# A two-layer transformer kernel: the experts' up weights loaded as one run of eight rows a partition

## The chip, the cores and the metric

The kernel runs on one NeuronCore of a Trainium2 chip. The metric is the device time of one execution in microseconds. Three runs of the kernel before gave 1952.04, 1953.3 and 1950.11 us, a median of 1952.04 us.

The core has five engines with a queue of instructions each: TensorE (PE; its weight loads are listed as PEld), VectorE (DVE), ScalarE (ACT), GpSimd (POOL) and SyncE (SP), which here only issues DMAs. Sixteen DMA engines move data between HBM and the on-chip memory SBUF, which has 128 partitions. Matrix products land in PSUM.

## The reference, cut to what matters

The program is two blocks of two layers each on a sequence of 256 tokens of 1024 float32 features. The first block has a mixer (convolutions in layer 0, attention in layer 1), a layer norm, and then a mixture of 32 experts of which every token uses two:

```python
h = x.reshape(-1, d)                                   # 256 tokens x 1024 features
# a group (1 of 4) and two of its 8 experts are chosen for each token
gate, up = jnp.split(jnp.matmul(xc, w_up[e]), 2, axis=-1)      # w_up[e]: 1024 x 1024
y = jnp.matmul(jax.nn.silu(gate) * up, w_down[e])              # w_down[e]: 512 x 1024
out = jnp.zeros((t, d), h.dtype).at[tok].add(y * weight)
```

All of the weights are float32 and are used once, so that both layers' expert weights come to 64 x (4 MB + 2 MB). The second block (two attention kinds, a gated feed-forward and a gate per layer) is not touched by the change.

A product over the 1024 features is a sum, and it may be taken in any order, as long as the token's features and the rows of `w_up[e]` are cut in the same way.

## The kernel before, in words

**Stages.** The program runs ten stages one after another: 0 convolutions, 1 experts of layer 0, 2 attention, 3 experts of layer 1, and 4 to 9 the second block.

**Weights.** All large weights are cut into items of 1 MB that go to tiles `w` of 128 partitions x 2048 floats. The list `items` has them in the order of use. `pump` (lines 195 to 208) issues the DMA of the next item on SP's queue (line 205) as soon as some tile of the pools is free, and `done` frees a tile when its last reader has been placed. During the expert stages up to 20 tiles circulate (pools of 7, 6, 4 and 3), so that SP can have many loads under way, over a stage's end too: the first experts' weights are asked for while the stage before still runs, and the next stage's weights while the last experts compute.

**An expert's items.** For each expert there are four items of the up weights and two of the down weights (lines 139 to 143). The function `rows` (line 69) maps row `k*128 + p` of the matrix to partition `p`, chunk `k`. An up item holds two chunks, so that each partition gets two pieces of 4096 bytes that lie 512 KB apart in HBM; the 128 pieces of a chunk lie one after another.

**The tokens' features.** The router (stages 1 and 3) scores the tokens, and `gather_mm` (line 822) picks the up to 32 tokens of each of four experts with matrix products: the stationary operand is a chunk of 128 features of the token matrix `x` (256 tokens as 2 x 128 partitions), the moving one is a 0/1 matrix. The result, features on partitions, tokens along the row, is copied out of PSUM by `put` (line 846) with the layer norm's gain and bias for each feature, which `fv` takes from `fvec`: a table that stage 0 makes by turning the loaded vectors (lines 333 to 335). `up` (line 882) then multiplies chunk after chunk with the weights (line 892); `turn` and `down` follow (lines 901 and 914).

**Order around a stage's start.** The router's last step on PE is the gather for the first four experts: eight products for the first 128 tokens, then, after a short step on DVE, eight for the others. Then comes `up(0)`, whose readings free the first tiles. Products of float32 stand as two records each in the trace, so that eight are 16 records.

Of the kernel before, what the change touches and what calls it, by code (L numbers as in the profile page):

```python
# [10 lines left out]
F32 = mybir.dt.float32  # L11
# [23 lines left out]
LN_MIX_G, LN_MIX_B, LN_FFN_G, LN_FFN_B, NORM = 0, 2, 4, 6, 8  # L35
# [33 lines left out]
def rows(ap):  # L69
    return ap.rearrange("(k p) n -> p k n", p=128)  # L70


@with_exitstack
def tile_kernel(ctx: ExitStack, tc: tile.TileContext, A, out, first=0, last=9):
    nc = tc.nc
    V, S, G, T, Q = nc.vector, nc.scalar, nc.gpsimd, nc.tensor, nc.sync
    NA, NB, NC, ND = 7, 6, 4, 3

    const = ctx.enter_context(tc.tile_pool(name="const", bufs=1))
# [7 lines left out]
    def bank():  # L87
        return psum.tile([128, 512], F32, name="ps", tag="ps")
# [4 lines left out]
    items, halves = [], []  # L93

    def dense(view, kind):
        items.append(view)
        i = len(items) - 1
        if kind in ("cols4", "cols2"):
            k = int(kind[4])
            n = 1024 // k  # L100
            for j in range(2):
                halves.append((i, (k, n), lambda t, j=j, k=k, n=n: t.rearrange("p (k n) -> p k n", k=k)
                               [:, :, j * n:(j + 1) * n]))
        elif kind == "feat":
            for m in range(2):
                halves.append((i, (8, 128), lambda t, m=m: t.rearrange("p (k n) -> p k n", k=8)
                               [:, :, m * 128:(m + 1) * 128]))
        elif kind == "gate":
            halves.append((i, (8, 112), lambda t: t[:, 0:896].rearrange("p (k n) -> p k n", k=8)))
        else:  # L110
            k, n = {"tok": (4, 256), "row": (1, 1024)}[kind]
            for j in range(2):
                halves.append((i, (k, n), lambda t, j=j, k=k: t[:, j * 1024:(j + 1) * 1024]
                               .rearrange("p (k n) -> p k n", k=k)))

    def cols(w, c0, n=256):
        return rows(w)[:, :, c0:c0 + n]

    def out_items(w, pairs=False):
        for j in range(0 if pairs else 2):  # L120
            dense(rows(w)[:, 0:4, j * 512:(j + 1) * 512], "cols4")
        for k in range(0 if pairs else 4, 8, 2):
            dense(rows(w)[:, k:k + 2, :], "cols2")
# [3 lines left out]
    for s in range(first, last + 1):  # L127
        stage_half[s] = len(halves)
        if s == 0:
            for i in range(2):  # L130
                dense(cols(A["even_w_in"][0], 2048 + 256 * i), "feat")
                dense(cols(A["even_w_in"][0], 1536 + 256 * i), "feat")
            for i in range(2):
                for c in (512, 1024, 0):
                    dense(cols(A["even_w_in"][0], c + 256 * i), "feat")
            out_items(A["even_w_out"][0])
        elif s in (1, 3):
            moe_items[s] = len(items)
            for e in range(NE):
                for k in range(4):  # L140
                    items.append(rows(A["expert_w_up"][s // 2, e])[:, 2 * k:2 * k + 2, :])
                for k in range(2):
                    items.append(rows(A["expert_w_down"][s // 2, e])[:, 2 * k:2 * k + 2, :])
        elif s == 2:
            for hg in range(4):
                dense(cols(A["odd_w_qkv"][0], 256 * hg), "feat")
                dense(cols(A["odd_w_qkv"][0], 1024 + 256 * hg), "feat")
                dense(cols(A["odd_w_qkv"][0], 2048 + 256 * hg), "tok")
            out_items(A["odd_w_o"][0])
        elif s == 4:  # L150
            for hg in range(4):
                for j in range(3):
                    dense(cols(A["w_in_ab_2"][0], (hg // 2) * 1536 + (hg % 2) * 256 + 512 * j), "tok")
            out_items(A["w_out_ab_2"][0], True)
        elif s in (5, 8):
            for f in range(NF + 1):
                if f < NF:
                    dense(cols(A["w_ffn_gate_2"][s // 7], 256 * f), "feat")
                    dense(cols(A["w_ffn_up_2"][s // 7], 256 * f), "feat")
                if f:  # L160
                    dense(rows(A["w_ffn_down_2"][s // 7])[:, 2 * f - 2:2 * f, :], "row")
        elif s in (6, 9):
            dense(rows(A["w_ple_proj_2"][s // 9]), "row")
            for u in range(4):
                dense(cols(A["w_ple_gate_2"][s // 9], 256 * u), "feat")
        else:
            w = A["w_in_nsa_2"][0]
            for j, n in enumerate(("k", "v")):
                dense(cols(w, 1024 + 256 * j), "tok")
            for n in ("k", "v"):  # L170
                items.append(A[f"cmp_{n}_w1_2"][0].rearrange("(l p) n -> p l n", p=128))
            for c in (1536, 2048):
                dense(cols(w, c), "tok")
            dense(cols(w, 2496, 112), "gate")
            for c in (0, 256, 1792, 2304, 512, 768):
                dense(cols(w, c), "tok")
            out_items(A["w_out_nsa_2"][0], True)
# [118 lines left out]
    x = const.tile([128, 2, D], F32, name="x")  # L296
# [17 lines left out]
    ident = const.tile([128, 128], F32, name="ident")  # L314
# [4 lines left out]

    fvec = const.tile([128, 8, 14], F32, name="fvec")  # L320

    def vector_loads(vr):
        lo, hi = (0 if first < 4 else 8), (14 if last > 3 else 8)
        for j, n in enumerate(("ln_mix_g", "ln_mix_b", "ln_ffn_g", "ln_ffn_b", "norm_mix_2", "norm_ffn_2",
                               "norm_ple_2")):
            if lo <= 2 * j < hi:
                Q.dma_start(vr[2 * j:2 * j + 2, :], A[n])
        if lo:
            V.memset(vr[0:8, :], 0.0)

        def go():
            ps = bank()
            for k in range(8):
                T.transpose(ps[:, k * 14:k * 14 + hi], vr[0:hi, k * 128:(k + 1) * 128], ident[:hi, :hi])
            V.tensor_copy(fvec[:, :, 0:hi], ps[:, 0:112].rearrange("p (k n) -> p k n", k=8)[:, :, 0:hi])
        return go

    def fv(j):
        return lambda k: fvec[:, k, j:j + 1]
# [201 lines left out]
    def conv_mix():  # L541
        mp = rt["pool"]
        with tc.tile_pool(name="cm", bufs=1, reuse_waits="tile") as cp:
# [9 lines left out]
            Q.dma_start(fvr[36:37, :], A["even_norm_b_b"])  # L553
            pump(1)
            vectors = vector_loads(vr)
            prep = router_loads(0)
            pump()
# [165 lines left out]
    def router(mp):  # L723
# [59 lines left out]
        def first():  # L783
            place(0)
            warm(8)
            gather_mm(pg, 0, dsp[:, 0, 0:4])
# [7 lines left out]
        place(1)  # L794
        warm(2)
        gather_mm(pg, 1, dsp[:, 1, 0:4])
        rt.update(pos=pos, first=pg, dt=dt)

# [23 lines left out]
    def gather_mm(ps, c, dsp):  # L822

        for k in range(8):
            T.matmul(ps[k // 4][:, k % 4 * 128:k % 4 * 128 + 128], x[:, c, k * 128:(k + 1) * 128],
                     dsp.rearrange("p e s -> p (e s)"), start=k % 4 == 0 and c == 0, stop=c == 1,
                     skip_group_check=True)

    def moe(layer):
        stage = 2 * layer + 1  # L830
        with tc.tile_pool(name="wd", bufs=ND, reuse_waits="tile") as wd, \
# [5 lines left out]
            router(mg)  # L837
            base = moe_items[stage]
            acc = [bank() for _ in range(4)]
            gain, bias = fv(LN_MIX_G + layer), fv(LN_MIX_B + layer)  # L840
            xgs, y4s, hts = {}, {}, {}
            dsp = rt["dt"][:, 0:512].rearrange("p (c e s) -> p c e s", c=2, e=8)
            dwt = rt["dt"][:, 512:].rearrange("p (q t) -> p q t", q=2)
# [22 lines left out]
            def gather(g, hb):  # L866
                ps = [bank(), bank()]
                for c in range(2):
                    gather_mm(ps, c, dsp[:, c, 4 * hb:4 * hb + 4])
                gathered(g, hb, ps)  # L870
# [1032 lines left out]
    def second_block():  # L1903
        nonlocal jdent, sm
        with tc.tile_pool(name="b2", bufs=1, reuse_waits="tile") as bp, tc.tile_pool(name="sm2", bufs=2) as sm:
# [20 lines left out]
            if first > 3:  # L1926
                with tc.tile_pool(name="b2c", bufs=1) as cp:
                    vector_loads(cp.tile([14, D], F32, name="vr"))()
                    block2_consts(*[cp.tile([128, D], F32, name=f"consts{j}") for j in range(2)])()
# [31 lines left out]
    if 7 in stage_half:  # L1961
        j = halves[stage_half[7]][0]
        nsa_w1 = {"k": j + 2, "v": j + 3}
    with ExitStack() as es:
        if first < 4:
            rt["pool"] = es.enter_context(tc.tile_pool(name="mp", bufs=1, reuse_waits="tile"))
            for p, n in (("b", NB), ("c", NC)):
                pools[p] = es.enter_context(tc.tile_pool(name="w" + p, bufs=n, reuse_waits="tile"))
                free.extend(p * n)
        for s in range(first, min(last, 3) + 1):  # L1970
            if s == 0:
                conv_mix()
            elif s == 2:
                stick_mix()
            else:
                moe(s // 2)
# [37 lines left out]
```

## Time and profile before

| What | Value |
|---|---|
| time, median of 3 runs | 1952.04 us (1950.11 to 1953.3) |
| the profiled execution | 1952.0 us, of which the span 1950.3 us |
| PE busy | 1638.0 us (84%) |
| DVE, ACT, POOL busy | 781.6, 681.3, 196.3 us |
| moved by DMA | 559.04 MB, mean 287 GB/s |
| issues of expert weights | 256 of up weights, 128 of down weights, 1024 KB each |

The page cuts the span into 40 slices of 48.8 us. The row DMA gives the share in tenths that the 16 DMA engines were busy, and the row GB/s what they moved. The expert stages are the two stretches of slices in which DMA shows 9 throughout: about 160 to 590 us, and 749 to 1180 us. Packets of one DMA engine overlap slightly in the records, so that a share can come out a little above 1.

### The profile page before, as it was taken

How to read it: one execution, taken by the hardware profiler on the slowest of the kernel's cores; microseconds unless marked ns; L12 is line 12 of the kernel's file. 1: busy time of each engine (PE TensorE's matmuls, PEld its weight loads, DVE VectorE, ACT ScalarE, POOL GpSimd, SP SyncE). 2: the span in 40 equal slices, each digit the busy share in tenths (PEclk: the TensorE clock that was granted, in tenths of full speed). 3: DMA queues.
4: the chain of work that ended last, by engine and by line, in shares of the span. 5: the costliest groups of instructions: out<-in, count | busy, mean ns of one | idle time of the engine just before them, and what ended most of it. 6: DMA issues, size and time to landing. Idle time of an engine off the chain costs nothing. (4 is left out here: it accounts for less than half of the span.)

```text
span 1950.3 us, 34572 instructions
## 1 busy us (share of the span) xinstructions
PE 1638.0 (84%) x14717; PEld 1241.2 (64%) x14717; DVE 781.6 (40%) x1569; ACT 681.3 (35%) x1299; POOL 196.3 (10%) x152
## 2 busy tenths in 40 slices
PE   7769767667668999767657778999999998999998
PEld 7756423224226986323324225999999997799998
DVE  5873100001104663100001004666655857666557
ACT  3423111111114663211111114655444646654445
POOL 4721000000001000000000002111000412110001
PEclk9889878778878999977778788999999999999999
DMA  9549999999999659999999999545555463145550
GB/s 299 213 143 394 418 419 418 418 420 418 418 419 349 241 182 362 418 420 419 418 418 419 419 419 310 161 154 179 180 186 178 140 207 112 55 136 195 192 176 23
DMA packets 236570, 559.04 MB, mean 287 GB/s; under 512 B 15563, under 2 KB 124938, under 8 KB 236408
## 3 DMA queue, kind: packets, MB, share of 16 engines
q1 hardware_dynamic: 226520, 551.59, 74.3%
q10 hardware_dynamic: 9264, 4.97, 0.9%
q8 instruction: 119, 1.95, 0.4%
q14 instruction: 43, 0.35, 0.1%
q0 software_dynamic: 624, 0.18, 0.0%
HBM read 555.55 MB, written 1.15 MB: 285 GB/s over the span
## 5 line engine op out<-in xcount | busy, mean ns | idle before, releaser
L892 PE MATMUL ps<-w,xg 128*32 128x256 f32 x4096 | 362.3, 493 | 235.8 <-DMA w<-in_expert_w_up_dram 231.5
L892 PEld LDWEIGHTS ps<-w,xg 128*32 128x32 f32 x4096 | 134.7, 132 | 445.5 <-DMA w<-in_expert_w_up_dram 266.2
L251 DVE TENSOR_TENSOR wl<-w,wh 128x1024 fp32r<-128x1024 f32 x231 | 281.2, 1226 | 157.2 <-ACT wh L240 153.9
L240 ACT ACTIVATE wh<-w 128x1024 fp32r<-128x1024 f32 x273 | 283.5, 1051 | 90.5 <-PE ps L401 60.1
L896 DVE TENSOR_TENSOR hs<-hs,ps 128x128 f32<-128x128 f32 x64 | 18.4, 288 | 631.6 <-ACT hs L895 631.6
L400 PE MATMUL ps<-xh,wh 128*128 128x256 f32 (+1 forms) x840 | 237.1, 282 | 0.0
L402 PE MATMUL ps<-xh,wl 128*128 128x256 f32 (+1 forms) x840 | 236.3, 281 | 0.8 <-DVE wl L251 0.8
L401 PE MATMUL ps<-xl,wh 128*128 128x256 f32 (+1 forms) x840 | 236.6, 282 | 0.4 <-DVE xl L1218 0.3
L895 ACT ACTIVATE hs<-ps 128x128 f32<-128x128 f32 x64 | 17.8, 278 | 591.9 <-PE ps L892 587.2
L251 POOL TENSOR_TENSOR wl<-w,wh 128x1024 fp32r<-128x1024 f32 x42 | 115.5, 2764 | 996.2 <-ACT wh L240 996.2
L402 PEld LDWEIGHTS ps<-xh,wl 128*128 128x128 f32 (+1 forms) x840 | 159.2, 189 | 1.2 <-DVE wl L251 1.2
L401 PEld LDWEIGHTS ps<-xl,wh 128*128 128x128 f32 (+1 forms) x840 | 159.2, 189 | 1.2 <-DVE xl L1218 1.2
L400 PEld LDWEIGHTS ps<-xh,wh 128*128 128x128 f32 (+1 forms) x840 | 159.2, 190 | 0.0
L914 PE MATMUL ps<-w,ht 128*32 128x256 f32 x2048 | 144.9, 432 | 0.0
L921 ACT ACTIVATE y<-ps 32x256 f32<-32x256 f32 x256 | 96.0, 375 | 119.9 <-PE ps L914 113.8
L914 PEld LDWEIGHTS ps<-w,ht 128*32 128x32 f32 x2048 | 74.5, 128 | 67.6 <-issue 35.7
L402 PE MATMUL ps<-wh,xl 128*128 128x256 f32 x352 | 100.4, 285 | 5.0 <-DVE xl L1218 5.0
L400 PE MATMUL ps<-wh,xh 128*128 128x256 f32 x352 | 102.2, 290 | 1.5 <-ACT xh L1215 1.5
L401 PE MATMUL ps<-wl,xh 128*128 128x256 f32 x352 | 99.6, 283 | 0.0
L401 PE MATMUL ps<-al,wh 128*128 128x256 f32 x352 | 99.1, 281 | 0.0
L400 PE MATMUL ps<-ah,wh 128*128 128x256 f32 x352 | 99.0, 281 | 0.0
L402 PE MATMUL ps<-ah,wl 128*128 128x256 f32 x352 | 99.0, 281 | 0.0
(403 smaller groups left out, 2883.5 us busy)
## 6 DMA issues: line engine op xcount, KB each, us to landing
w<-in_expert_w_up_dram SPq DMA_DIRECT2D x256, 1024.0 KB
w<-in_expert_w_down_dram SPq DMA_DIRECT2D x128, 1024.0 KB
w<-in_w_ffn_gate_dram SPq DMA_DIRECT2D x22, 1024.0 KB
w<-in_w_ffn_up_dram SPq DMA_DIRECT2D x22, 1024.0 KB
w<-in_w_ffn_down_dram SPq DMA_DIRECT2D x22, 1024.0 KB
w<-in_odd_w_qkv_dram SPq DMA_DIRECT2D x12, 1024.0 KB
w<-in_w_in_ab_dram SPq DMA_DIRECT2D x12, 1024.0 KB
w<-in_w_in_nsa_dram SPq DMA_DIRECT2D x10, 1024.0 KB
```

Of the source, the lines that this page charges most:

```text
L240: S.activation(hv, src, AF.Copy)
L251: eng.tensor_tensor(out=lv, in0=src, in1=hv.bitcast(F32), op=OP.subtract)
L400: T.matmul(ps, lh, rh, start=start, stop=False, **kw)
L401: T.matmul(ps, lh, rl, start=False, stop=False, **kw)
L402: T.matmul(ps, ll, rh, start=False, stop=stop, **kw)
L892: T.matmul(pu[32 * j:32 * j + 32, 0:256], r, w[:, kk, :, j, :], start=k == 0, stop=k == 7)
L895: S.activation(hs, pu[:, 0:128], AF.Silu)
L896: V.tensor_tensor(out=hs, in0=hs, in1=pu[:, 128:256], op=OP.mult)
L914: T.matmul(pd[32 * c:32 * c + 32, 0:256], hts[e][:, 32 * j:32 * j + 32], w[:, jj, c * 256:(c + 1) * 256], start=j == 0, stop=j == 3)
L921: S.activation(y4s[q][32 * ee:32 * ee + 32, c * 256:(c + 1) * 256], pd[32 * c:32 * c + 32, 0:256], AF.Copy)
```

## The change

The up weights' rows are dealt to the partitions in another way: partition `p` gets the eight neighbouring rows `8p` to `8p+7` (new function `runs`). An item still holds two of the eight, and these are now one piece of 8192 bytes; the next partition's piece lies 32 KB further on. The down weights stay as they are.

Chunk `k` of the features is then `k, k+8, k+16, ...` in place of 128 neighbours. So the gather reads its stationary operand with a step of eight floats (32 bytes), and the gain and bias for the gathered features come from a second small table, `runvec`, which is made by eight further transposes and a copy in stage 0.

```diff
+def runs(ap):
+
+    return ap.rearrange("(p k) n -> p k n", p=128)
...
-                    items.append(rows(A["expert_w_up"][s // 2, e])[:, 2 * k:2 * k + 2, :])
+                    items.append(runs(A["expert_w_up"][s // 2, e])[:, 2 * k:2 * k + 2, :])
...
+    runvec = const.tile([128, 8, 4], F32, name="runvec") if first < 4 else None
...
             V.tensor_copy(fvec[:, :, 0:hi], ps[:, 0:112].rearrange("p (k n) -> p k n", k=8)[:, :, 0:hi])
+            if not lo:
+                ps = bank()
+                for k in range(8):
+                    T.transpose(ps[:, k * 4:k * 4 + 4], vr[0:4, k::8], ident[:4, :4])
+                V.tensor_copy(runvec.rearrange("p k n -> p (k n)"), ps[:, 0:32])
...
     def gather_mm(ps, c, dsp):
...
-            T.matmul(ps[k // 4][:, k % 4 * 128:k % 4 * 128 + 128], x[:, c, k * 128:(k + 1) * 128],
+            T.matmul(ps[k // 4][:, k % 4 * 128:k % 4 * 128 + 128], x[:, c, k::8],
...
-            gain, bias = fv(LN_MIX_G + layer), fv(LN_MIX_B + layer)
+            gain, bias = [lambda k, j=j + layer: runvec[:, k, j:j + 1] for j in (LN_MIX_G, LN_MIX_B)]
```

On SP's queue, where the first experts' weights follow those of stage 0, the kernel before has these rows (the tile `w`, what it is loaded from, and the shape of the access):

```order
L205 DMA w<-in_even_w_in_dram 128x8x256 x6
L205 DMA w<-in_even_w_out_dram 128x4x512 x2
L205 DMA w<-in_even_w_out_dram 128x2x1024 x2
L205 DMA w<-in_expert_w_up_dram 128x2x1024 x4
L205 DMA w<-in_expert_w_down_dram 128x2x1024 x2
```

and the changed one, whose lines of the same functions stand some lines lower, has these:

```order
L210 DMA w<-in_even_w_in_dram 128x8x256 x6
L210 DMA w<-in_even_w_out_dram 128x4x512 x2
L210 DMA w<-in_even_w_out_dram 128x2x1024 x2
L210 DMA w<-in_expert_w_up_dram 128x2048 x4
L210 DMA w<-in_expert_w_down_dram 128x2x1024 x2
```

The number of DMAs and their order are the same; an up item is 128 pieces of 2048 floats in place of 128 x 2 pieces of 1024. On PE in stage 0, between two products of the convolution's input (lines 400 to 402), the table `fvec` is turned out of the loaded vectors `scr`:

```order
L401 MATMUL ps<-w,wh 128x256
L402 MATMUL ps<-w,wl 128x256
L334 MATMUL ps<-ident,scr 128x14 x8
L400 MATMUL ps<-w,wh 128x256
L401 MATMUL ps<-w,wh 128x256
```

and in the changed kernel:

```order
L413 MATMUL ps<-w,wh 128x256
L414 MATMUL ps<-w,wl 128x256
L341 MATMUL ps<-ident,scr 128x14 x8
L346 MATMUL ps<-ident,scr 128x4 x8
L412 MATMUL ps<-w,wh 128x256
L413 MATMUL ps<-w,wh 128x256
```

Eight transposes are added behind the eight that were there, and on DVE one copy behind that of line 335. Elsewhere the instructions and their order are the same; of the gathers and the copies behind them only the addresses change.

## Rows read from the trace of the kernel before

**Rows 1.** The page: the span in 40 slices, and the DMA packets.
```profile
PE   7769767667668999767657778999999998999998
...
DMA  9549999999999659999999999545555463145550
GB/s 299 213 143 394 418 419 418 418 420 418 418 419 349 241 182 362 418 420 419 418 418 419 419 419 310 161 154 179 180 186 178 140 207 112 55 136 195 192 176 23
DMA packets 236570, 559.04 MB, mean 287 GB/s; under 512 B 15563, under 2 KB 124938, under 8 KB 236408
...
q8 instruction: 119, 1.95, 0.4%
q14 instruction: 43, 0.35, 0.1%
```

**Rows 2.** Waits of the whole span: engine, line, releaser, us, times, longest.
```profile
PEld ps L892 <- DMA w<-in_expert_w_up_dram: 266.2, 162, 4.7
PE ps L892 <- DMA w<-in_expert_w_up_dram: 231.5, 186, 6.0
```

**Rows 3.** Busy time by stretch; the last two columns are DMA share and GB/s.
```profile
161.00:575.00 414.00, 297.85 (x3201) 140.81 (x3189) 40.09 (x123) 67.76 (x182) 3.46 (x6) 0.81 1.02 418
300.00:500.00 200.00, 141.39 (x1457) 65.71 (x1457) 19.77 (x53) 29.74 (x82) 0.00 (x0) 0.78 1.03 418
749.00:1170.00 421.00, 300.62 (x3265) 142.67 (x3257) 38.91 (x120) 69.36 (x187) 0.00 (x0) 0.81 1.02 417
622.00:630.00 8.00, 8.00 (x80) 7.79 (x79) 3.42 (x5) 3.24 (x4) 0.00 (x0) 1.00 1.09 386
```

**Rows 4.** DMA issues from 159.3 to 600 us (first two alike in 748 to 1190).
```profile
w<-in_expert_w_up_dram SPq DMA_DIRECT2D x114, 1024.0 KB
w<-in_expert_w_down_dram SPq DMA_DIRECT2D x58, 1024.0 KB
w<-in_odd_w_qkv_dram SPq DMA_DIRECT2D x4, 1024.0 KB
```

**Rows 5.** PE in order of time at stage 1's start: start, us, line, operands, count.
```profile
146.37 1.98 PE L739 MATMUL ps<-rw,xt 128*128 128x36 f32 x16
148.17 1.07 PE L508 MATMUL ps<-ident,x 128*128 128x128 f32 x8
...
153.55 2.05 PE L825 MATMUL ps<-dt,x 128*128 128x128 f32 x16
155.44 0.59 PE L396 MATMUL ps<-onesb 128*128 128x512 bf16 x2
155.87 0.18 PE L777 MATMUL ps<-mb,onesb 128*128 128x32 bf16 x1
...
156.69 2.05 PE L825 MATMUL ps<-dt,x 128*128 128x128 f32 x16 [0.18 <-DVE dt L780]
158.68 3.66 PE L892 MATMUL ps<-w,xg 128*32 128x256 f32 x64
```

**Rows 6.** SP's queue: issues of weights at the two expert stages' starts.
```profile
159.81 1.23 SPq L205 DMA_DIRECT2D w<-in_expert_w_up_dram  x2
161.53 1.26 SPq L205 DMA_DIRECT2D w<-in_expert_w_down_dram  x2
...
748.49 1.23 SPq L205 DMA_DIRECT2D w<-in_expert_w_up_dram  x2
```

**Rows 7.** Busy time by stretch around these issues; last columns DMA share, GB/s.
```profile
155.00:159.00 4.00, 3.82 (x36) 2.88 (x38) 0.91 (x4) 1.11 (x4) 0.88 (x2) 1.00 1.03 416
159.00:160.00 1.00, 1.00 (x25) 0.57 (x21) 1.00 (x4) 0.40 (x2) 0.00 (x0) 1.00 0.22 74
...
748.00:749.00 1.00, 1.00 (x24) 0.62 (x20) 0.84 (x3) 0.98 (x2) 0.00 (x0) 1.00 0.07 29
```

**Rows 8.** PE around 1570 us: products with a moving operand at a step.
```profile
1570.68 4.57 PE L1658 MATMUL ps<-kpk,w 128*128 128x75 f32 x32
1574.98 0.39 PE L400 MATMUL ps<-wh,xh 128*128 128x256 f32 x1
```

**Rows 9.** Weight loads, whole span, shapes apart: busy us, mean ns, idle before.
```profile
L825 PEld LDWEIGHTS ps<-dt,x 128*128 128x128 f32 x512 | 59.4, 193 | 2.1 <-DVE dt L780 2.1
L508 PEld LDWEIGHTS ps<-ident,xn 128*128 128x128 f32 x16 | 1.7, 141 | 0.8 <-DVE xn L496 0.8
L716 PEld LDWEIGHTS ps<-rw,fvec 128*1 128x1 f32 x32 | 1.1, 85 | 0.3
```

**Rows 10.** PE, then DVE, in order of time in stage 0.
```profile
23.84 0.80 PE L334 MATMUL ps<-ident,scr 14*128 14x14 f32 x8
24.57 0.39 PE L400 MATMUL ps<-w,wh 128*128 128x256 f32 x1
...
27.78 0.69 DVE L615 TENSOR_TENSOR gp<-sg,ps 128x512 f32<-128x512 f32 x1 [2.82 <-PE ps L402]
29.20 19.02 DVE L590 SCALAR_TENSOR_TENSOR scr<-gp,vec,scr 128x256 f32<-128x256 f32 x26 [0.73 <-DMA w<-in_even_w_in_dram]
```

**Rows 11.** One stretch late in stage 0.
```profile
100.00:110.00 10.00, 0.00 (x0) 0.00 (x0) 9.42 (x18) 2.80 (x4) 3.39 (x2) 0.64 0.00 0
```

## The prediction

> **What bounds the kernel now.** I read the 40 slices first. In slices 5 to 12 and 17 to 24 the DMA row shows 9 and the GB/s row 418 to 420, while PE shows 6 to 8 [rows 1]: these are the two expert stages, and there the loads are the bound. The waits say the same: PE's products of line 892 waited 231.5 us in all for up weights [rows 2]. By stretch, 161 to 575 and 749 to 1170 us have a DMA share of 1.02 at 417 to 418 GB/s with PE busy for 298 of 414 and 301 of 421 us [rows 3]. So a tile of 1.049 MB takes 1.049/418 = 2.51 us, PE has over a quarter of its time to spare, and what the loads lose or gain in these stretches goes through to the end. Outside them the weights run ahead and PE, or in stage 0 DVE, sets the pace.
>
> **The change, part by part.**
>
> *The loads.* In each stage 114 up tiles are issued after the stretch has begun [rows 4]; the other 14 come earlier, with DMA time to spare. So 228 tiles count. What a longer piece is worth I take from two saturated stretches. Around 626 us only next-stage weights in pieces of 1 KB arrive: 386 GB/s at share 1.09. Between 300 and 500 us everything comes in pieces of 4 KB: 418 GB/s [rows 3]. An engine has a sixteenth of that, so a piece takes 1024 x 16/386 = 42.4 ns and 4096 x 16/418 = 156.8 ns. The line through both has 38.1 ns per KB and 4.3 ns per piece. A piece of 8 KB then takes 309.3 ns against 313.6 for two of 4 KB, 1.4% less: 34 ns a tile, and 228 x 34 ns = 7.8 us gained.
>
> Its ends: the row of before has no load of weights in pieces over 4 KB (only the 162 packets of the two instruction queues are above 8 KB [rows 1]), so nothing shows that SP's queue moves 8 KB as one packet. If not, the gain is 0. If the busy shares are taken for the packets' real time (16 x 1.09/386 gives 46.3 ns per 1 KB, 16 x 1.03/418 gives 161.5 per 4 KB), 8 KB take 315.1 against 323.0 ns, 2.4%: 14 us gained. A loss is possible too, through the new addresses; it is the third rival. I take the middle value, since it goes by bytes that arrived and not by shares over 1.
>
> *The gathers.* 512 records of line 825 [rows 9] now read the stationary operand at a step of 32 bytes. Most of them lie in the stretches where PE waits for weights: a gather of 32 records that grew by 3 us would still be hidden by up to 20 tiles on their way. Only the first gather of each stage counts in full. Its two halves of 16 records stand on PE without a break but for 0.18 us, right before `up(0)` [rows 5], and SP's next loads come only when `up(0)` frees tiles: at 159.8 us, a microsecond after its start at 158.7 [rows 6]; the same holds at 748.5. Just then the DMA has run dry: its share falls from 1.03 to 0.22 at 159 us, and to 0.07 at 748 [rows 7]. So 64 records stand on the path, and each nanosecond more on one is 0.064 us.
>
> What a record costs is set by the weight load: 16 records of line 739 with only 36 moving columns take 148.17 - 146.37 = 1.80 us, 112 ns each, and those of line 825 take 1.89/16 = 118 ns [rows 5]. No weight load at a step is in the trace, so I bound it. Line 1658 reads its moving operand at the same step, eight floats: 32 records in 4.30 us, 134 ns for 75 columns, 1.79 ns a column [rows 8], where line 825 has at most 118/128 = 0.92. A read at this step therefore costs at least 1.94 times as much. If a weight load grows alike, 112 becomes 217 ns and the two first gathers lose 64 x 0.105 = 6.7 us. Against it: a block of the same 128 x 128 floats is loaded for a transpose in 141 ns and for a product in 193, and a single column takes 85 [rows 9]. So reading 128 contiguous columns needs at most 56 ns, and the load for a product takes 108 above the single column; a read 1.94 times as long, 109 ns, would just fit in. I take 0, because these rows are weight loads themselves, and keep 6.7 as the other end. A gain has no ground: the operand has as many columns as before.
>
> [...]
>
> *Stage 0.* The eight transposes of line 334 took 24.57 - 23.84 = 0.73 us on PE. DVE was waiting 2.82 us for PE's next result and then ran unbroken [rows 10]; late in the stage it is DVE that everyone waits for (9.42 of 10 us busy while PE has none) [rows 11]. So eight more delay the chain by about 0.7 us; the bounds are 0, if a later wait takes them up, and 1.5, if the read at a step doubles them. The copy to `runvec` lies in DVE's wait.
>
> *Neither adds nor removes anything:* the copies with gain and bias have the same shapes, and SP issues the same DMAs in the same order.
>
> *Sum:* 1952.0 (the profiled execution: span 1950.3 and 1.7 around it; the median of the runs is 1952.04) - 7.8 + 0 + 0.7 = 1944.9 us, 0.36% less.
>
> **The rivals.**
>
> 1. *The gathers give it back.* The loads gain 7.8 us, but weight loads at a step take 217 ns: -7.8 + 6.7 + 0.7, 1951.6 us. For it speaks line 1658, against it the quick weight loads of the transposes.
>
> 2. *The change doesn't do what it says on the wires.* The queue cuts 8 KB into two packets of 4 KB. The rate stays at 418 and only stage 0's transposes are left: 1952.7 us; with rival 1's gathers on top, 1959.4. For it: queue 1 shows no packet of 8 KB or more. Against it: packets of 1.95 MB/119 = 16 KB exist on the instruction queue [rows 1].
>
> 3. *Slower: the new addresses.* Before, the 128 pieces of a chunk make one solid block of 512 KB. Now 128 pieces lie at a pitch of 32 KB, a power of two, and engines that advance in step could meet in the same part of HBM. Every per cent of rate costs 228 x 25 ns = 5.7 us, and the kernel is slower beyond the bound from a loss of 0.6%. If the rate fell to that of the 1 KB pieces, 386 GB/s, it would be 228 x 2.51 x 8.3% = 47 us: some 2000 us. For it speaks nothing in the rows; against it, that the loads around 626 us read at a pitch too (12 KB, the rows of `odd_w_qkv`) and keep all engines busy, share 1.09 [rows 3]. [...]
>
> 4. *More gained.* The pieces' overhead is as large as the busy shares make it: 1952.0 - 14 + 0.7 = 1938.7 us.
>
> **How the numbers follow.** Forecast 0.42, gathers 0.26, cut packets 0.10, new addresses 0.15, more gained 0.07. The two with a gain of more than 0.2% (3.9 us, about what a measurement of this kernel can tell from no change) are the forecast and the last, 0.49; 0.03 of it I give to sums that end short of the bound: faster 0.46. Within the bound end rival 1 less 0.02 (gathers that cost still more), rival 2 less 0.03 (with dear gathers on top), and that 0.03: 0.34. Slower are the addresses and the 0.05 taken from rivals 1 and 2: 0.20. The range reaches from 1938 (the larger gain) to 1960 (cut packets with dear gathers); beyond it lies nearly all of the addresses' case. The forecast's own range is 1941 to 1948.
>
> **What would show it.** In the changed profile: the number of packets falls by 256 x 128 = 32768, and the stretch 300 to 500 us shows about 422 GB/s in place of 418 (down tiles stay at 4 KB). If the count stays, it is rival 2; if the rate falls, rival 3. The first gather's 16 records still take 1.9 us and the weight load 193 ns; if they take 3.5 us and some 300 ns, rival 1 is right. Line 334's successors start the next product 0.7 us later. The forecast is wrong if the DMA share of the expert stages drops below 1, since then something other than the loads would be the bound.

## The result and the profile after

The changed kernel takes 1963.99 us (median of 4 runs, 1962.1 to 1966.56) where the kernel before took 1951.76 in the same comparison: 12.2 us more, a ratio of 1.0065 with a 95% interval of 1.0051 to 1.0079. It is slower, since the whole interval lies above 1, and the time lies above the forecast's range of 1938 to 1960. The profiled execution took 1962.1 us, with a span of 1960.5.

The page of the changed kernel, DMA and GB/s in 40 slices, and the packets:

```profile
DMA  9538999999999758999999999445555463245550
GB/s 289 216 148 361 415 416 416 417 417 416 417 416 341 268 189 323 416 417 416 416 417 417 417 416 343 157 140 170 194 180 191 141 198 108 66 134 195 186 180 23
DMA packets 203802, 559.04 MB, mean 285 GB/s; under 512 B 15563, under 2 KB 124938, under 8 KB 170872
```

Against [rows 1] there are 236570 - 203802 = 32768 packets fewer, as many as 8 KB pieces should save, so the queue does move 8 KB as one packet. But the expert stages, which showed 418 to 420 GB/s, now show 415 to 417. The same by stretch (columns as in [rows 3]; the last two are DMA share and GB/s), each stretch moved so that it begins after the stage's new start:

```profile
166.00:580.00 414.00, 315.45 (x3193) 170.12 (x3189) 39.99 (x123) 67.75 (x182) 3.45 (x6) 0.84 1.02 416
300.00:500.00 200.00, 149.54 (x1425) 81.68 (x1425) 19.08 (x52) 29.73 (x82) 0.00 (x0) 0.81 1.02 417
757.00:1180.00 423.00, 322.31 (x3264) 171.38 (x3256) 39.28 (x122) 68.28 (x184) 0.00 (x0) 0.82 1.01 415
```

The DMA share is still above 1, so the loads are still the bound, and PE still has time to spare (315 of 414 us). What the loads bring per microsecond fell by 0.2 to 0.5%, where a rise of 1% was forecast. PE's waits for up weights, line 904 for line 892 of [rows 2]:

```profile
PEld ps L904 <- DMA w<-in_expert_w_up_dram: 206.7, 131, 3.7
PE ps L904 <- DMA w<-in_expert_w_up_dram: 192.8, 150, 5.8
```

PE waits less (192.8 us for 231.5), yet the kernel is longer: PE itself became busier. Its gathers, in order of time at the start of stage 1, and then the weight loads of the gathers over the whole span (these answer to [rows 5] and [rows 9]):

```profile
154.42 4.08 PE L837 MATMUL ps<-dt,x 128*128 128x128 f32 x16
158.34 0.59 PE L408 MATMUL ps<-onesb 128*128 128x512 bf16 x2
158.77 0.18 PE L789 MATMUL ps<-mb,onesb 128*128 128x32 bf16 x1
...
159.59 4.09 PE L837 MATMUL ps<-dt,x 128*128 128x128 f32 x16 [0.18 <-DVE dt L792]
163.61 3.66 PE L904 MATMUL ps<-w,xg 128*32 128x256 f32 x64
```

```profile
L837 PEld LDWEIGHTS ps<-dt,x 128*128 128x128 f32 x512 | 124.1, 336 | 2.1 <-DVE dt L792 2.1
```

A half gather of 16 records takes 4.08 us in place of 2.05, and a weight load 336 ns in place of 193. From the first half's start to `up(0)` it is 163.61 - 154.42 = 9.19 us; in [rows 5] it was 158.68 - 153.55 = 5.13. That is 4.06 us. At the start of stage 3 the same two marks, the first half's start and `up(0)`, stand in the kernel before and in the changed one at

```profile
742.24 2.05 PE L825 MATMUL ps<-dt,x 128*128 128x128 f32 x16
747.36 1.93 PE L892 MATMUL ps<-w,xg 128*32 128x256 f32 x32
...
746.99 4.08 PE L837 MATMUL ps<-dt,x 128*128 128x128 f32 x16
756.18 1.07 PE L904 MATMUL ps<-w,xg 128*32 128x256 f32 x16
```

which is 9.19 us in place of 5.12, so that both stages make 8.1 us. The DMA has run dry meanwhile, as the prediction said it would; the stretch from the last arrival to the next issue answers to [rows 7], where such a stretch was under a microsecond:

```profile
159.92:164.13 4.21, 4.21 (x28) 3.92 (x31) 0.41 (x2) 1.51 (x4) 0.00 (x0) 1.00 0.02 5
```

4.21 us at a share of 0.02. Only when `up(0)` frees tiles do SP's next issues come (164.74 us, against 159.81 in [rows 6]):

```profile
164.74 1.19 SPq L210 DMA_DIRECT2D w<-in_expert_w_up_dram  x2
```

In stage 0 the eight new transposes (line 346) stand between those of [rows 10] and the next product:

```profile
24.43 0.69 PE L341 MATMUL ps<-ident,scr 14*128 14x14 f32 x8
24.97 1.02 PE L346 MATMUL ps<-ident,scr 4*128 4x4 f32 x8
25.92 0.39 PE L412 MATMUL ps<-w,wh 128*128 128x256 f32 x1
```

From the first transpose to that product it is 25.92 - 24.43 = 1.49 us, where [rows 10] have 0.73: 0.76 us more.

So the profile shows two things to explain: gathers that cost twice as much, and a rate that fell where it should have risen.

### The profile page after: what moved, and what is told of

Its sections match the earlier page's. It is cut to its first block, busy times and chain, and to the rows that moved or that the text cites. A ratio compares the mean times of both kernels' runs of the same rounds, so it can differ in the third digit from the quotient of the medians.

```text
span 1960.5 us, 34589 instructions
## 1 busy us (share of the span) xinstructions
PE 1684.6 (86%) x14725; PEld 1305.1 (67%) x14725; DVE 781.1 (40%) x1570; ACT 681.3 (35%) x1299; POOL 196.3 (10%) x152
## 2 busy tenths in 40 slices
DMA packets 203802, 559.04 MB, mean 285 GB/s; under 512 B 15563, under 2 KB 124938, under 8 KB 170872
## 5 line engine op out<-in xcount | busy, mean ns | idle before, releaser
L904 PE MATMUL ps<-w,xg 128*32 128x256 f32 x4096 | 349.2, 485 | 198.3 <-DMA w<-in_expert_w_up_dram 192.8
L412 PEld LDWEIGHTS ps<-xh,wh 128*128 128x128 f32 (+1 forms) x840 | 159.3, 190 | 0.0
L837 PE MATMUL ps<-dt,x 128*128 128x128 f32 x512 | 125.3, 402 | 0.4 <-DVE dt L792 0.4
L837 PEld LDWEIGHTS ps<-dt,x 128*128 128x128 f32 x512 | 124.1, 336 | 2.1 <-DVE dt L792 2.1
```

The lines of the kernel that those rows point to most:

```text
L412: T.matmul(ps, lh, rh, start=start, stop=False, **kw)
L904: T.matmul(pu[32 * j:32 * j + 32, 0:256], r, w[:, kk, :, j, :], start=k == 0, stop=k == 7)
```

## The experiments

All are compared with the kernel before on the same chip; its medians there were 1951.12, 1951.18 and 1952.14 us in the three groups. Where one row stands under an experiment it is its stretch from 300 to 500 us, columns as above, and the number to read is the last, GB/s. The profiled execution is one of the runs and not always the middle one: in e2_loads_only it took 1939.74 us and in e7_pairs_aligned 1942.74, each the fastest of its group.

### The two halves of the change

The first two kernels leave out the match of features and weight rows, so that what they compute isn't the reference's result; only their time is read.

**Gathers alone** (e1_gather_only): the loads of before, the gathers and `runvec` of the changed kernel. Part of its diff against the kernel before:

```diff
+    runvec = const.tile([128, 8, 4], F32, name="runvec") if first < 4 else None
...
-            T.matmul(ps[k // 4][:, k % 4 * 128:k % 4 * 128 + 128], x[:, c, k * 128:(k + 1) * 128],
+            T.matmul(ps[k // 4][:, k % 4 * 128:k % 4 * 128 + 128], x[:, c, k::8],
...
```

> The loads are those of before (pieces of 4 KB), the gather and its gain/bias table those of after; the features that meet the weights are not the matching ones. Theory 1 (the gather makes most of the loss): 64 records on the path at 238 in place of 112 ns give 8.1 us, the extra transposes 0.9 us: 1959 to 1962 us, expert stretches at 417 to 418 GB/s, weight loads 336 ns. Rival (the loads make the loss, the gather's longer records are mostly covered): 1952 to 1955 us.

```profile
300.00:500.00 200.00, 145.00 (x1409) 78.80 (x1401) 17.26 (x49) 29.68 (x82) 0.00 (x0) 0.82 1.03 409
```

1981.1 us, ratio 1.0155 (1.0138 to 1.0172): 30 us slower, and a miss: 19 us above the nearer theory's range and 26 above the other's. The loads are those of before, and yet the rate is 409 GB/s in place of 418.

**Loads alone** (e2_loads_only): 8 KB pieces, the gathers of before, no `runvec`. Part of its diff:

```diff
-                    items.append(rows(A["expert_w_up"][s // 2, e])[:, 2 * k:2 * k + 2, :])
+                    items.append(runs(A["expert_w_up"][s // 2, e])[:, 2 * k:2 * k + 2, :])
```

> The loads are those of after (pieces of 8 KB, 32 KB apart), gather and table those of before; the features that meet the weights are not the matching ones. Theory 1 (the new loads are a little slower, 415.5 against 417.4 GB/s over some 840 us of expert stretches, 0.45%): +2 to +4 us, 1954 to 1956. Rival (the loads gain 4 to 8 us as predicted, and the gather hides it by delaying the stream): 1944 to 1948 us at 421 GB/s or more.

```profile
300.00:500.00 200.00, 141.91 (x1492) 66.95 (x1481) 20.32 (x55) 30.49 (x85) 0.00 (x0) 0.80 1.02 423
```

1944.98 us, ratio 0.9965 (0.995 to 0.9979); the five runs spread from 1939.74 to 1946.27. The rate is 423 GB/s at the same pitch of 32 KB as in the changed kernel. So the longer pieces bring what was forecast, the new addresses in HBM cost nothing, and whatever lowers the rate came with the other half of the change.

### Shorter runs

Runs of R neighbouring rows in place of eight: with R = 2 (e3_pairs) an up item is one solid megabyte of 8 KB pieces and the gather steps by 8 bytes; with R = 4 (e4_quads) the pitch is 16 KB and the step 16 bytes.

```diff
+R = 2
...
+    g, r = divmod(k, R)
+    return ap.rearrange("(g p r) n -> g p r n", p=128, r=R)[g][:, r:r + 2, :]
...
-                    T.transpose(ps[:, k * 4:k * 4 + 4], vr[0:4, k::8], ident[:4, :4])
+                    T.transpose(ps[:, k * 4:k * 4 + 4], vr[0:4, chunk(k)], ident[:4, :4])
...
-            T.matmul(ps[k // 4][:, k % 4 * 128:k % 4 * 128 + 128], x[:, c, k::8],
+            T.matmul(ps[k // 4][:, k % 4 * 128:k % 4 * 128 + 128], x[:, c, chunk(k)],
```

> Runs of two rows: an item is again one solid block of 1 MB, partition p gets rows 2p and 2p+1 of it, pieces of 8 KB at a pitch of 8 KB; the gather steps by two floats (8 bytes). Theory P (the pitch of 32 KB ate the gain of the long pieces): 421 to 423 GB/s in 300 to 500 us, 4 KB packets back at 159 ns, time 1944 to 1947 if the gather costs what it did before. Theory C (418 GB/s is a ceiling of the path whatever the piece): 417 to 418 GB/s, 8 KB packets over 309 ns, time 1951 to 1954. [...]

For R = 2 the half gathers and the start of `up(0)`, the weight loads, and the rate:

```profile
156.00 2.15 PE L845 MATMUL ps<-dt,x 128*128 128x128 f32 x16
159.24 2.15 PE L845 MATMUL ps<-dt,x 128*128 128x128 f32 x16 [0.18 <-DVE dt L800]
161.32 1.05 PE L912 MATMUL ps<-w,xg 128*32 128x256 f32 x13
```

```profile
L845 PEld LDWEIGHTS ps<-dt,x 128*128 128x128 f32 x512 | 62.5, 198 | 2.1 <-DVE dt L800 2.1
```

```profile
300.00:500.00 200.00, 138.15 (x1433) 66.11 (x1437) 19.75 (x53) 29.67 (x82) 0.00 (x0) 0.80 1.02 417
```

1957.27 us, ratio 1.0029 (1.0017 to 1.004). A step of two floats is nearly free: 2.15 us for 16 records, 198 ns a weight load. But the rate is 417 GB/s, as low as with the pitch of 32 KB. Theory P missed. Theory C has the rate, but its time (1951 to 1954) is missed, and its ground, a ceiling of the path whatever the piece, is refuted by the 423 GB/s of the loads alone.

For R = 4:

> Runs of four rows: pieces of 8 KB at a pitch of 16 KB, gather at a step of four floats (16 bytes). Theory P: a rate between that of the pairs and 415.5 GB/s; theory C: 417 to 418 GB/s as all others. [...]

```profile
155.17 4.00 PE L845 MATMUL ps<-dt,x 128*128 128x128 f32 x16
160.25 4.00 PE L845 MATMUL ps<-dt,x 128*128 128x128 f32 x16 [0.17 <-DVE dt L800]
164.19 2.15 PE L912 MATMUL ps<-w,xg 128*32 128x256 f32 x36
```

```profile
L845 PEld LDWEIGHTS ps<-dt,x 128*128 128x128 f32 x512 | 121.4, 330 | 2.1 <-DVE dt L800 2.1
```

```profile
300.00:500.00 200.00, 152.24 (x1438) 82.01 (x1430) 17.97 (x51) 31.23 (x86) 0.00 (x0) 0.80 1.02 417
```

1966.17 us, ratio 1.0082 (1.0065 to 1.0098). It is 8.9 us more than with R = 2, at the same rate of 417 GB/s. At 16 bytes the gather is as slow as at 32 (4.00 against 4.08 us), so between these two the cost hardly grows with the step. The weight loads say the same: 193 ns for neighbours, 198 at a step of 8 bytes, 330 at 16 and 336 at 32, so nearly all of the price comes between 8 and 16 bytes. What in the read makes it no run shows.

Four kernels now had the low rate: gathers alone, R = 2, R = 4 and the changed kernel. They differ in pitch, step and length of the pieces. What they share, and the loads alone lack, is a gather at a step, the eight new transposes, and the tile `runvec`. The next two experiments tell these apart. `runvec` takes 128 bytes a partition of the constants' pool, and all pools behind it move by as much. By the addresses that the build gave them, 7 weight tiles stood 224 bytes past a multiple of 256 in the kernel before and 13 on one; with `runvec` they stand 96 and 128 bytes past one.

### The place of the tiles

**The changed kernel with the shift made 256 bytes** (e5_after_aligned). Nothing else differs but two small tiles of the router put into one, to make room.

```diff
-    runvec = const.tile([128, 8, 4], F32, name="runvec") if first < 4 else None
+    runvec = const.tile([128, 64], F32, name="runvec")[:, 0:32].rearrange("p (k n) -> p k n", k=8)
```

> The changed kernel, with the new runvec tile made 256 bytes a partition instead of 128 (only its first 128 are used), so that all weight tiles behind it move by 256 bytes against the kernel before instead of 128 (two small tiles of the router share one to make room). Address theory: what slowed the transfers of every run that carries runvec is the 128-byte shift of their targets; here the expert stretches go back to 421 to 423 GB/s with 8 KB pieces of 309 ns as in e2_loads_only, the gathers stay slow (period near 238 ns, up of the first expert starting near 163 us), and the time is 1950 to 1954 us. Gather theory: the strided gathers themselves, or the runvec arithmetic, disturb the transfers; the rate stays at 415 to 416 GB/s and the time at 1963 to 1966 us.

```profile
300.00:500.00 200.00, 151.39 (x1445) 81.61 (x1449) 19.74 (x53) 29.79 (x83) 0.00 (x0) 0.81 1.02 423
```

```profile
155.04 4.07 PE L838 MATMUL ps<-dt,x 128*128 128x128 f32 x16
160.21 4.07 PE L838 MATMUL ps<-dt,x 128*128 128x128 f32 x16 [0.18 <-DVE dt L792]
164.21 2.15 PE L905 MATMUL ps<-w,xg 128*32 128x256 f32 x36
```

1951.98 us, ratio 1.0002 (0.9993 to 1.0012). The rate is back at 423 GB/s while the gathers stay at 4.07 us: they don't disturb the loads. The shift was worth 1963.99 - 1951.98 = 12.0 us.

**The kernel before with a shift of 128 bytes** (e6_before_shift) by an unused tile, and nothing else:

```diff
+    const.tile([128, 32], F32, name="pad")
```

> The kernel before with nothing changed but an unused tile of 128 bytes a partition at the end of the constants, which moves all weight tiles by 128 bytes. Address theory: the expert stretches fall from 418 to about 407 GB/s, 4 KB pieces take 164 ns instead of 160, as in e1_gather_only, and the time is 1968 to 1974 us. Gather theory: nothing moves, 1950 to 1953 us.

```profile
300.00:500.00 200.00, 140.18 (x1425) 65.75 (x1425) 18.04 (x51) 29.68 (x82) 0.00 (x0) 0.78 1.03 409
```

1971.42 us, ratio 1.0107 (1.009 to 1.0124). A tile that no instruction touches makes the kernel 20 us slower. With this the cause is shown from both sides. It also answers e1_gather_only: 20.2 us for the shift, 8.1 for the gathers and 0.8 for the transposes are 29.1 of its 30.0.

**Runs of two rows, shift of 256** (e7_pairs_aligned): the third experiment with the same line of diff as the fifth.

> e3_pairs (runs of two rows, 8 KB pieces, gather of every second feature) with runvec made 256 bytes as in e5_after_aligned. Address theory: 421 to 423 GB/s in the expert stretches, gather period near 117 ns, up of the first expert near 157 to 158 us, 1943 to 1948 us, faster than the kernel before. Gather theory: as e3_pairs, 415 to 416 GB/s and 1956 to 1958 us.

```profile
300.00:500.00 200.00, 141.40 (x1469) 67.15 (x1473) 19.73 (x53) 29.67 (x82) 0.00 (x0) 0.80 1.02 422
```

1946.85 us, ratio 0.9978 (0.9969 to 0.9988), as expected: 10.4 us less than with the shift of 128. Against the loads alone, gathers and `runvec` still cost 1946.85 - 1944.98 = 1.9 us, which is not clear of the spread of these two groups (1942.74 to 1950.22 here).

**The kernel before with all 20 tiles on a multiple of 256** (e8_all_aligned), by 32 unused bytes in the constants and 224 behind the first weight pool (two small tiles share one again):

```diff
+    const.tile([128, 8], F32, name="pad")
...
+            rt["pool"].tile([128, 56], F32, name="pad2")
```

> The kernel before (4 KB pieces) with unused padding of 32 and of 224 bytes a partition ahead of two pools, so that the 7 weight tiles that stood 32 bytes short of a multiple of 256 stand on one too, as the other 13 already do. If a target off a multiple of 256 bytes costs by itself, those 7 tiles cost already in the kernel before, and the rate rises from 418 to 419 to 423 GB/s, the time falls to 1938 to 1948 us. If only some offsets (128 and 96) cost, nothing moves: 418 GB/s, 1950 to 1953 us.

```profile
300.00:500.00 200.00, 143.83 (x1477) 67.39 (x1481) 20.02 (x54) 30.01 (x83) 0.00 (x0) 0.78 1.03 420
```

1945.93 us, ratio 0.9976 (0.9966 to 0.9985). The 7 tiles had cost something already in the kernel before: 5.3 us.

Do 224 bytes past a multiple cost less than the other offsets? The traces can tell. From 9 to 14 us the loads of `even_w_in` go in pieces of 1 KB to these 7 tiles alone. In that stretch e8_all_aligned, the kernel before (224 bytes past), and two later experiments (32 and 128 past) have

```profile
9.00:14.00 5.00, 5.00 (x31) 4.76 (x31) 2.98 (x4) 3.61 (x5) 1.68 (x1) 1.00 1.09 386
9.00:14.00 5.00, 5.00 (x25) 4.76 (x24) 2.81 (x4) 3.44 (x5) 1.68 (x1) 1.00 1.09 347
9.00:14.00 5.00, 5.00 (x30) 4.76 (x30) 2.87 (x4) 3.50 (x5) 1.80 (x1) 1.00 1.09 346
9.00:14.00 5.00, 5.00 (x36) 4.77 (x35) 2.98 (x4) 3.55 (x5) 1.75 (x1) 1.00 1.10 346
```

So 224 bytes cost as much as 32 or 128: an engine's 1 KB piece takes 1024 x 16/386 = 42.4 ns on a multiple and 47.2 off it. The loss is there before PE reads its first weight at 9.74 us (382 against 320 GB/s from 8.3 to 9.7 us), so PE's reading of the same tiles is not what makes it.

### The version that both findings give, and the offset

**Runs of two rows, all tiles on a multiple of 256** (e9_pairs_all_aligned); `runvec` lies in the 224 bytes behind the first weight pool.

```diff
+    const.tile([128, 8], F32, name="pad")
...
+            rt["runvec"] = rt["pool"].tile([128, 56], F32, name="runvec")[:, 0:32]
```

> e7_pairs_aligned with all 20 weight tiles on a multiple of 256 bytes: 32 unused bytes at the end of the constants, and runvec in a 224-byte tile behind the first weight pool, so that it fills the gap that e8_all_aligned left unused. If the two gains add (8 KB pieces: e2_loads_only took 6.1 us off; all tiles aligned: e8_all_aligned took 5.3 us off; the gather of every second feature costs 1.9 us more than that of neighbours, e7 against e2): 1940 to 1942 us, 422 to 423 GB/s, pieces of 309 ns. If longer pieces and aligned tiles remove the same loss: 1945 to 1947 us, as e7_pairs_aligned.

```profile
300.00:500.00 200.00, 145.17 (x1492) 68.93 (x1493) 20.32 (x55) 30.49 (x85) 0.00 (x0) 0.78 1.02 424
```

1939.25 us, ratio 0.9934 (0.992 to 0.9947): faster than both kernels, 12.9 us below the one before and 24.7 below the change as it was made. It is just below the expected 1940 to 1942. The gains add; the single ones make 6.1 + 5.3 - 1.9 = 9.5 us, and the 3.4 us beyond that are less than the spread within the groups that they come from.

**All tiles 128, 64 or 32 bytes past a multiple of 256** (e10_all_128, e11_all_64, e12_all_32), from the kernel with all of them on one; the diff shows the first (24 and 16 floats in the others), and six small tiles of the router share one for room.

```diff
-    const.tile([128, 8], F32, name="pad")
+    const.tile([128, 40], F32, name="pad")
```

> e8_all_aligned with all weight tiles moved by a further 128 bytes (unused padding; six small tiles of the router share one to make room). 4 KB pieces. In e6_before_shift, with 13 tiles at 128 and 7 at 96 bytes past a multiple of 256, the rate was 407 GB/s and the time 20 us above before. Theory A (any offset from 256 costs the same): 407 GB/s, 1969 to 1974 us. Theory B (the cost goes by the offset, and 128 is the worst): 404 to 407 GB/s, 1970 to 1978 us. Theory C (the 7 tiles at 96 carried the loss): 418 GB/s, 1944 to 1950 us.

```profile
300.00:500.00 200.00, 140.85 (x1422) 66.57 (x1423) 17.09 (x49) 28.53 (x79) 0.00 (x0) 0.77 1.03 409
```

> As e10_all_128, with all weight tiles 64 bytes past a multiple of 256. Theory A: 407 GB/s, 1969 to 1974 us, as e10. Theory B: between, 409 to 415 GB/s and 1952 to 1966 us. Theory C (multiples of 64 cost nothing): 418 GB/s, 1944 to 1950 us.

```profile
300.00:500.00 200.00, 134.99 (x1412) 64.11 (x1416) 17.09 (x49) 29.29 (x81) 0.00 (x0) 0.80 1.02 409
```

> As e10_all_128, with all weight tiles 32 bytes past a multiple of 256. Theory A: 407 GB/s, 1969 to 1974 us. Theory B: nearest to aligned, 414 to 418 GB/s, 1946 to 1956 us (in the kernel before 7 of 20 tiles stood 32 bytes short of a multiple, and aligning them gave 5.3 us: all 20 would cost some 15 us, 1961 us, if 32 past costs as 32 short does). Theory C (offsets that are no multiple of 64 are those that cost): 407 GB/s or less.

```profile
300.00:500.00 200.00, 136.68 (x1409) 64.51 (x1412) 17.26 (x49) 29.63 (x82) 0.00 (x0) 0.78 1.02 409
```

| tiles past a multiple of 256 | us | ratio, 95% interval |
|---|---|---|
| 128 bytes | 1972.35 | 1.0102 (1.0086 to 1.0117) |
| 64 bytes | 1972.24 | 1.01 (1.0084 to 1.0115) |
| 32 bytes | 1974.41 | 1.0112 (1.0097 to 1.0128) |

Theory A: any of these offsets costs the same (its times hold, the last but for 0.4 us; the rate is 409 where it had 407). An engine's 4 KB piece takes 4096 x 16/420 = 156.0 ns on a multiple and 4096 x 16/409 = 160.2 off it: 4.2 ns a piece. The two stages have 384 items of 256 pieces, 6144 pieces an engine, so 25.8 us; measured, 1972.35 - 1945.93 = 26.4. With 8 KB pieces for the up weights, two of 8 KB and two of 4 KB take 24576 x 16/424 = 927.4 ns against 943.0 at 417 GB/s: 3.9 ns a piece, for 4096 pieces 16.0 us, where R = 2 measured 1957.27 - 1939.25 = 18.0. The packet records from 300 to 500 us agree: a 4 KB packet took 159.4 ns on average in e8_all_aligned and 163.6 to 163.7 in the three kernels of the table, an 8 KB packet 309.7 in e9_pairs_all_aligned and 314.5 in e3_pairs. The price goes by pieces, not by bytes: by bytes R = 2 would have lost the same 26 us.

In these runs it is the target in SBUF that moves. What in the write costs these 4 ns no run shows.

## Why the prediction was wrong

- *What bounds the kernel*: right. The DMA share stays above 1, and every change of the rate in the experiments came out at the end.
- *The loads, -7.8 us*: right in mechanism and nearly in size. Alone they gave 6.1 us (1951.12 to 1944.98) at 423 GB/s, where some 422 were forecast. Rivals 2 and 3, cut packets and new addresses, are refuted by the packet count and by that rate at a pitch of 32 KB (423 again with the gathers of the change, in e5_after_aligned). The sign given for rival 3, a rate that falls, came true, but from another cause.
- *The gathers, 0*: wrong; the step that failed is the choice between the bounds. The transposes' load of 141 ns and the single column's 85 [rows 9] were read as room into which a slow read would fit. There was none: the load grew by 143 ns, and 16 records from 2.05 to 4.08 us. The row to go by was line 1658 [rows 8], the only one with a read at a step, with its factor of 1.94. Gathers and stage 0 together cost 1951.98 - 1944.98 = 7.0 us by the medians, and 8.1 + 0.8 = 8.9 by the rows; rival 1 had 7.4. The spread of e2_loads_only leaves the 7.0, and the 6.1 of the loads, uncertain by some 2 us. That rival's sum, 1951.6, is within half a microsecond of the changed kernel with a shift of 256; its mechanism was right, so close a number is in part luck.
- *Stage 0, +0.7 us*: right at its place, where PE's next product comes 0.76 us later. What is left of it at the end no run shows by itself: the first gather starts 0.87 us later (154.42 in place of 153.55), but between kernels whose stage 0 has the same instructions this start differs by more (151.15 in e8_all_aligned, 155.22 in e12_all_32).
- *"Neither adds nor removes anything"*: here is the step that made the sign wrong. `runvec` was priced by its instructions and not by its place. A term is missing from the sum: 12.0 us for the 128 bytes by which it moved the targets of all weight loads. No rival had it, and the third, the only one on the slower side, put the loss of rate at the source in HBM, where it isn't (423 GB/s with the new addresses in e2_loads_only, 409 with the old ones in e6_before_shift).

Put together: 1952.0 - 6.1 + 7.0 + 12.0 = 1964.9 us, against 1964.0 measured. This closes by construction, since the terms are steps from the kernel before over e2_loads_only and e5_after_aligned to the changed kernel. What stands by itself is the price of the 128 bytes without any other part of the change, 20.2 us with 4 KB pieces: by pieces that makes two thirds, 13.5 us, for the changed kernel (measured 12.0, and 10.4 with R = 2).

What stays open: the kernel before has 7 of 20 tiles off, and 138 of the 384 expert items go into them (36%), but aligning them gave only 5.3 of the 26.4 us that all 20 cost. The offset of 224 bytes is not the reason, by the rows from 9 to 14 us; whether pieces off a multiple cost less when most others are on one was not tried. With 8 KB pieces the same step, e7_pairs_aligned to e9_pairs_all_aligned, gave 7.6 of 18.0 us, which is no less than their share.

## What to carry to other kernels

Where loads are the bound, look at where a new tile pushes the targets of the loads, not only at what it holds: a few idle bytes that keep them on multiples of 256 were worth more here (12.0 us in the changed kernel) than the longer pieces themselves (6.1 us). A stationary operand may be read at a step of two floats for almost nothing (198 ns a weight load against 193), but at four or eight its load took 1.7 times as long (330 and 336 ns); choose the shortest runs that give the piece its length. A slower instruction counts in full where the loads wait for it, even if the same instruction is hidden everywhere else: of the 512 slower records here, the 64 at the two stages' starts made 8.1 us.

## What the runs showed of the hardware that was not expected

- A DMA piece whose target in SBUF lies off a multiple of 256 bytes takes some 4 to 5 ns longer, whether it has 1, 4 or 8 KB, and with 4 KB pieces whether it is off by 32, 64 or 128: 420 against 409 GB/s with pieces of 4 KB, 386 against 346 or 347 with pieces of 1 KB (off by 32, 128 or 224), and 424 against 417 with up weights in pieces of 8 KB (off by 96 or 128).
- A weight load of 128 columns of fp32 takes 193 ns for neighbours, 198 at a step of 8 bytes, 330 at 16 and 336 at 32.
- On aligned targets, up weights in 8 KB pieces raise the rate of the mixed stretch from 420 to 424 GB/s; with 7 of the 20 tiles off, as before, a pitch of 32 KB between pieces costs nothing (423 GB/s in e5_after_aligned, against 422 at a pitch of 8 KB in e7_pairs_aligned).
